# Hybrid attention and gMLP block: second chunk's tokens for z reloaded as rows and split, branch weights on GpSimd's queue, transposes moved, z's tiles where w_out's rows go later

## The chip, the cores and the metric

The kernel runs on one core of a Trainium2 chip. The metric is the device time of one execution in microseconds (us). The core has five instruction queues, each in order: PE (TensorE, matmuls and transposes), DVE (VectorE), ACT (ScalarE), POOL (GpSimd) and SP (SyncE, which only issues DMA transfers here). ACT and POOL can issue DMA transfers too. A core has 16 DMA engines that all queues share.

## What is computed

One decoder block on 2048 tokens of 1024 channels, all in float32. Cut to what matters here:

```python
h = _rmsnorm(x, norm_pre_mix[layer])
proj = jnp.einsum('bsd,de->bse', h, w_in[layer])
q, k, v = ...                                   # 12 heads of 64, rope on q and k
u = jax.nn.gelu(proj[..., U0:Z0])               # 512 channels
z = jax.nn.gelu(proj[..., Z0:GA0])              # 512 channels
gate_a = jax.nn.sigmoid(proj[..., GA0:GB0])     # 1024 channels
gate_b = jax.nn.sigmoid(proj[..., GB0:IN_WIDTH])
y_attn = _mixer_dilated_attention(q, k, v)      # 3 patterns, joined by their log-denominators
y_gmlp = _mixer_chunked_gmlp(u, z, ...)         # u * (tril(w_spatial) @ layernorm(z) + b_spatial)
merged = (gate_a * jnp.einsum('bse,ed->bsd', y_attn, w_branch_attn[layer])
          + gate_b * jnp.einsum('bse,ed->bsd', y_gmlp, w_branch_gmlp[layer]))
y = jnp.einsum('bsd,de->bse', merged, w_out[layer])
x = x + _rmsnorm(y, norm_post_mix[layer])
...                                             # squared-ReLU MLP of width 4096
```

## The kernel before

**Numbers.** Every large product is made from operands split in two: a high part (a rounded copy) and a low part (the operand less its high part). `mm3` multiplies high x high, high x low and low x high (L95, L96, L97). `split` makes the parts with one engine for the copy (L70 on ACT, L72 on POOL) and one for the difference (L78 on DVE or POOL). With `split` a raw float32 tile becomes a tile of two planes.

**Tokens.** There are four chunks of 512 tokens, 0 to 3. The normed tokens, transposed, lie in HBM twice: as raw float32 rows (`hT_d`, called hTd, 512 KB for two of the eight channel groups) and already split into two planes (`hb_d`, called hbd, twice the bytes). `reload_h(c)` makes a tile hT_b of chunk c and returns eight loads from hbd, one for two channel groups of one plane.

**The stretch around the change.** After q, k, v, u and the first half of z come the gate products (L707) in the generator `gates`: half 1 (chunks 2 and 3) and then half 0, each in seven products per block n of weight columns, numbered i = 1 to 7. Products 1 and 2 of one n use one PSUM bank: the bank is copied to x after product 1 (L726 or L728), and product 2 is added on top of it, so PE's product 2 needs that copy done. The weights of each product come through small tiles (gr, ga, cv) that are split into "spots". Attention's units run between them on all engines, a few matmuls at a time.

The order of all this is written by hand: `filler` is one long generator that yields after every three matmuls (a step), and `steps(n)` runs n of them between other work. `with behind():` puts instructions of ACT, DVE, POOL and SP behind the last one issued so far on the same engine, so that the scheduler keeps the written order.

- `combine(c)` joins attention's three patterns for one chunk: loads (A, or cw for chunk 1), statistics (L970 to L983), scaling (L988 on ACT, L991 on DVE), two adds (L993, L994), then eight transposes on PE (L999), copies and stores. `combined(...)` advances the combines of chunks 2, 3 and 0 with pairs (steps to run first, which combine). The combine of chunk 1 (the fourth) is advanced by `todo` in the loop at the end of `attention`'s function.
- Then z of half 0: `z_chunk` for chunk 0 and then chunk 1, four blocks of 128 tokens each, eight steps for a block. Each block's gelu is L572. The loads of chunk 1's tokens are in `zin`, one issued after each step. The same loop loads and splits the six branch weights (wbraw, wb; `load_wb`, `split_wb`), at steps listed in tuples.
- Then the merges. `merge(c, ...)` multiplies attention's and gMLP's outputs (yt) with the branch weights (b), and the gates (g, loaded from HBM by `load_gate`, sigmoid L1166) with these (L1183). The rows of w_out (woraw, wo) are loaded and split in the first merge (chunk 2), each row's load waiting for the place of an earlier one. The tiles woraw2, woraw3, woraw6 and woraw7 come from a pool (ttp) that lies where z's pool (zp0) was. `sz_out` finishes the gMLP branch of a chunk (L551 on PE, L558 and L561), writing sb tiles.
- `out_block` multiplies with w_out; with the first of the four blocks of a chunk the next chunk's yt and eight of its gates are loaded.

Of the kernel before, what the change touches and what calls it, by code (L numbers as in the profile page):

```python
# [41 lines left out]
def block_kernel(ctx, tc, a, out):  # L42
# [478 lines left out]
    def spatial(zp, half):  # L521

        wsp = zp.tile([P, 4, P], F32, name=f"wsp{half}", tag="wsp")
        bsp = zp.tile([P, 4, P], F32, name=f"bsp{half}", tag="bsp")
        lngb = zp.tile([P, 2, 32], F32, name=f"lngb{half}", tag="lngb")[:, :, :4]
        ones = st.tile([P, P], F32, name=f"ones{half}", tag="ones", bufs=1)
        sp.dma_start(wsp, a["w_spatial"])
# [135 lines left out]
    def gates():  # L663
# [12 lines left out]
        for t, (half, i, n) in enumerate(seq):  # L676
# [45 lines left out]
            for _ in range(2 if half and i == 4 or t in (LAST + 5, LAST + 7) else 1):  # L722
                if ins:
                    sp.dma_start(*ins.pop(0))
            if i == 1 and half and n > 1:
                dve.tensor_copy(x, p)  # L726
            elif i == 1:
                act.activation(x, p, AF.Copy)  # L728
# [38 lines left out]
    def filler():  # L767

        for q, (wi, kind, n, half) in enumerate(queue):
# [15 lines left out]
            if kind == "z":  # L785
                if not half:
                    zin.extend(reload_h(1))
                for ci in range(2):
                    yield from paced(z_chunk(zps[half], w, half * 2 + ci))
                    if half and not ci:  # L790
                        gates_ahead()
                continue
# [264 lines left out]
    def combined(*order):  # L1057
        for n, k in order:
            steps(n)
            with behind():  # L1060
                next(cs[k])

    combined((0, 0), (4, 1), (10, 0), (3, 0), (3, 0), (2, 2), (8, 0), (0, 1), (3, 1), (3, 1), (10, 1),
             (0, 2), (3, 2), (3, 2), (10, 2))
    steps(75 - 62)
    ec.close()
# [7 lines left out]
    def load_wb(k):  # L1074
        wb_raw[k] = wp.tile([P, D], F32, name=f"wbraw{k}", tag="raw", bufs=2)
        sp.dma_start(wb_raw[k], a["w_branch"][:, k, :])

# [8 lines left out]
    while not cw:  # L1086
        steps(1)
    todo = {14: (3,), 16: (3,), 18: (3,), 28: (3,)}
    for n in range(1, 56):
        steps(1)  # L1090
        if zin:
            sp.dma_start(*zin.pop(0))
        if n in (20, 24, 30, 34, 44, 50):
            split_wb((20, 24, 30, 34, 44, 50).index(n))
        if n in (6, 9, 20, 24, 30, 34):
            load_wb((6, 9, 20, 24, 30, 34).index(n))
        if n == 48:
# [71 lines left out]
    def merge(c, yt, between, each=None):  # L1169
        cs = slice(c * 512, (c + 1) * 512)  # L1170
        mg = []
        for dt in range(KT):
# [14 lines left out]
            if c != 2:  # L1187
                load_gate(c, dt + 5, 0)
                load_gate(c, dt + 3, 1)
            if dt < KT - 1:  # L1190
                for wch in range(2):
# [308 lines left out]
    for n, c in enumerate(chunks):  # L1500
        if n:
            mg = merge(c, yt, {0: flush, 2: flush}, merge_sums if c == 0 else merge_sums_last if c == 1 else None)
        for i in range(4):
# [5 lines left out]
            if n < 3 and not i:  # L1509
                yt = load_y(chunks[n + 1])  # L1510
                for dt, wch in ((0, 0), (0, 1), (1, 0), (1, 1), (2, 0), (2, 1), (3, 0), (4, 0)):
                    load_gate(chunks[n + 1], dt, wch)
            if n == 3 and i == 1:
# [562 lines left out]
```

## Time and profile before

| | |
|---|---|
| Median of 3 runs | 2667.13 us (2666.18 to 2668.09) |
| Profiled execution | 2667.0 us, span of its instructions 2665.1 us |
| TensorE clock granted, mean | 0.993 of full speed |
| ACT, POOL busy | 41%, 45% of the span |
| DMA, mean | 198 GB/s, 528.29 MB in all |

Times within the profile count from the span's start. The stretch that the change touches lies between 535 and 560 us (the first attention units) and between 970 and 1135 us (combines, z, first merge). In a list of waits a row says: engine and operation that waited, the line, what released it, then total us, number and longest. In a timeline a row gives start, duration, engine, line, operation, output and inputs, and in brackets how long the engine had stood idle and what ended that. Rows of windows give, for each engine, busy time and instructions, then the granted TensorE clock, the mean busy share of the DMA engines and GB/s. Rows of DMA issues end with the median us from issue to landing. "issue" as a releaser means that the profile shows none.

### The profile page before, as it was taken

The page shows a single profiled execution, that of the slowest core. Times are in us where ns is not written, and L with a number is a line of the kernel's source. Part 1 is how long each engine was busy: PE and PEld are TensorE (multiplying, and loading weights), DVE is VectorE, ACT ScalarE, POOL GpSimd, SP SyncE. Part 2 cuts the span into 40 slices and gives each one's busy share as a digit, 9 for nine tenths or more (in the row PEclk, how much of TensorE's full clock was granted, in tenths as well). Part 3 has the DMA queues.
Part 4 walks back from the last instruction along what each step waited for, and adds up shares of the span by engine and source line. Part 5 has one row for each costly group of instructions (what it writes and reads, how often), then busy time and mean ns, then how long its engine had stood idle before and what let it go on. Part 6 is the DMA issues. An engine that isn't in the chain of part 4 may idle for free. (4 is left out here: it accounts for less than half of the span.)

```text
span 2665.1 us, 35494 instructions
## 1 busy us (share of the span) xinstructions
PE 2622.6 (98%) x12458; PEld 2190.0 (82%) x12458; DVE 1657.0 (62%) x2799; ACT 1085.6 (41%) x2273; POOL 1192.4 (45%) x1089
## 2 busy tenths in 40 slices
PE   9999999999999998899999999999999999999998
PEld 8888888878888877688888888888888888888886
DVE  5676665544443455755676654655437888888866
ACT  5213111244445433444445555655545333223334
POOL 0363354365455552310334563223215776676644
PEclk9999999999999999899999999999999999999999
DMA  8779768888898899743656464643343212222235
GB/s 314 284 246 327 262 228 289 296 258 256 286 294 234 242 299 315 252 152 136 213 208 258 137 229 151 214 153 119 111 154 107 87 64 79 87 87 88 87 113 211
DMA packets 389860, 528.29 MB, mean 198 GB/s; under 512 B 57073, under 2 KB 242161, under 8 KB 388658
## 3 DMA queue, kind: packets, MB, share of 16 engines
q1 hardware_dynamic: 300912, 436.03, 49.7%
q0 software_dynamic: 14992, 51.65, 5.1%
q10 hardware_dynamic: 73778, 38.35, 4.7%
q8 instruction: 98, 1.61, 0.2%
q14 instruction: 80, 0.66, 0.1%
HBM read 342.77 MB, written 183.17 MB: 197 GB/s over the span
## 5 line engine op out<-in xcount | busy, mean ns | idle before, releaser
L1927 PE MATMUL ya<-T_spots,s 128*128 128x512 f32 x1176 | 289.2, 389 | 0.7 <-ACT T_spots L70 0.6
L70 ACT ACTIVATE s<-sraw 128x768 fp32r<-128x768 f32 (+1 forms) x184 | 127.2, 696 | 330.2 <-POOL sraw L1728 155.9
L1927 PEld LDWEIGHTS ya<-T_spots,s 128*128 128x128 f32 x1176 | 220.6, 188 | 47.3 <-ACT T_spots L70 1.0
L78 DVE TENSOR_TENSOR s<-sraw,s 128x512 fp32r<-128x512 f32 x172 | 184.2, 1095 | 8.6 <-ACT s L70 5.9
L1399 PE MATMUL aa<-B,A 128*128 128x512 f32 x768 | 182.2, 390 | 0.3 <-ACT xs L1413 0.3
L1370 POOL TENSOR_TENSOR s<-w1r 128x512 f32<-128x512 f32 x32 | 43.2, 1351 | 309.5 <-DVE S L78 271.8
L707 PE MATMUL g<-opA,spots 128*128 128x512 f32 x672 | 171.9, 400 | 0.0
L1399 PEld LDWEIGHTS aa<-B,A 128*128 128x128 f32 x768 | 143.9, 188 | 30.7 <-ACT xs L1413 1.0
L707 PE MATMUL g<-opB,spots 128*128 128x512 f32 x648 | 165.6, 400 | 0.0
L1927 PE MATMUL yc<-T_spots,s 128*128 128x512 f32 x624 | 159.6, 389 | 0.0
L95 PE MATMUL x<-hT_a,wq 128*128 128x512 f32 x384 | 149.7, 390 | 0.0
L96 PE MATMUL x<-hT_a,wq 128*128 128x512 f32 x384 | 149.4, 389 | 0.0
L97 PE MATMUL x<-hT_a,wq 128*128 128x512 f32 x384 | 149.4, 389 | 0.0
L707 PEld LDWEIGHTS g<-opA,spots 128*128 128x128 f32 x672 | 122.2, 190 | 22.1
L1927 PEld LDWEIGHTS yc<-T_spots,s 128*128 128x128 f32 x624 | 117.1, 188 | 24.3
L707 PEld LDWEIGHTS g<-opB,spots 128*128 128x128 f32 x648 | 118.0, 190 | 21.5
L78 POOL TENSOR_TENSOR spots<-gr,spots 128x512 fp32r<-128x512 f32 x98 | 126.6, 1295 | 17.7 <-ACT spots L70 8.3
L70 ACT ACTIVATE hl<-r 128x512 fp32r<-128x512 f32 x48 | 30.4, 633 | 235.3 <-POOL r L321 89.0
L1727 POOL TENSOR_TENSOR sraw<-sraw 128x256 f32<-128x256 f32 x56 | 41.9, 747 | 161.6 <-DVE s L78 158.6
L958 DVE TENSOR_REDUCE o<-po 128x256 f32<-128x512 f32 x48 | 33.2, 692 | 130.0 <-PE po L957 130.0
L72 POOL TENSOR_SCALAR spots<-gr 128x512 fp32r<-128x512 f32 x86 | 53.4, 621 | 133.8 <-PE g L707 96.2
L78 POOL TENSOR_TENSOR T_spots<-w2r,T_spots 128x512 fp32r<-128x512 f32 x70 | 104.5, 1520 | 7.3 <-ACT T_spots L70 7.3
(426 smaller groups left out, 6964.1 us busy)
## 6 DMA issues: line engine op xcount, KB each, us to landing
w1r<-in_w_mlp_in_dram SPq DMA_DIRECT2D x64, 512.0 KB, 3.7
sraw<-sd SPq DMA_DIRECT2D x128, 256.0 KB, 3.2
qk<-hl SPq DMA_DIRECT2D x24, 1024.0 KB, 5.6
qq<-qk SPq DMA_DIRECT2D x96, 256.0 KB, 5.1
w2r<-in_w_mlp_out_dram SPq DMA_DIRECT2D x16, 1024.0 KB, 7.6
sd<-u ACTq DMA_DIRECT2D x63, 256.0 KB, 3.1
g<-gated SPq DMA_DIRECT2D x58, 256.0 KB, 3.9
gr<-sgd SPq DMA_DIRECT2D x53, 256.0 KB, 4.7
```

Source lines behind the costliest of these rows:

```text
L70: act.activation(hi, src, AF.Copy)
L72: pool.tensor_scalar(hi, src, 1.0, 1.0, op0=OP.mult, op1=OP.mult)
L78: (pool if lo_eng == "pool" else dve).tensor_sub(lo, src, f32(hi))
L95: pe.matmul(ps, lh, rh, start=start, stop=False)
L96: pe.matmul(ps, lh, rl, start=False, stop=False)
L97: pe.matmul(ps, ll, rh, start=False, stop=stop)
L707: pe.matmul(p, w[:, l, k], h[:, r, k], start=i in (1, 6, 5, 4) and not k and not m, stop=k == 3 and m == 2, skip_group_check=True)
L958: dve.tensor_reduce(ot[:, :, j * 64:(j + 1) * 64], po.rearrange("p (b h e) -> p b e h", b=4, h=2), axis=AX.X, op=OP.add)
L1370: pool.tensor_add(s1, a21, a22)
L1399: pe.matmul(p, w[:, l, k, :], h[:, r, k, :], start=i in (1, 6, 5) and not k and not n, stop=k == 3 and n == 2, skip_group_check=True)
L1727: pool.tensor_add(a22, a21, a22)
L1927: pe.matmul(p, s[:, l], w[r], start=i in (1, 2, 5) and not m and not o, stop=m == 1 and o == 2, skip_group_check=True)
```

## The change

```diff
--- before.py
+++ after.py
@@ -523,6 +523,9 @@
         wsp = zp.tile([P, 4, P], F32, name=f"wsp{half}", tag="wsp")
         bsp = zp.tile([P, 4, P], F32, name=f"bsp{half}", tag="bsp")
         lngb = zp.tile([P, 2, 32], F32, name=f"lngb{half}", tag="lngb")[:, :, :4]
+        if not half:
+            zp.tile([P, 512], F32, name="sb_place", tag="sz", bufs=5)
+            zp.tile([P, 512], F32, name="ur_place", tag="ur", bufs=4)
         ones = st.tile([P, P], F32, name=f"ones{half}", tag="ones", bufs=1)
         sp.dma_start(wsp, a["w_spatial"])
         sp.dma_start(lngb[:, 0, :], a["ln_v_gain"])
@@ -722,9 +725,7 @@
             for _ in range(2 if half and i == 4 or t in (LAST + 5, LAST + 7) else 1):
                 if ins:
                     sp.dma_start(*ins.pop(0))
-            if i == 1 and half and n > 1:
-                dve.tensor_copy(x, p)
-            elif i == 1:
+            if i == 1:
                 act.activation(x, p, AF.Copy)
             elif i == 2:
                 act.activation(z, p, fn)
@@ -784,7 +785,8 @@
             w = loaded[q]
             if kind == "z":
                 if not half:
-                    zin.extend(reload_h(1))
+                    hT[1] = hp.tile([P, 2, KT, 512], F32R, name="hT_b1", tag="hT", bufs=2)
+                    zin.extend((f32(hT[1])[:, 1, k:k + 2], hT_d[1][:, k:k + 2]) for k in range(0, KT, 2))
                 for ci in range(2):
                     yield from paced(z_chunk(zps[half], w, half * 2 + ci))
                     if half and not ci:
@@ -1060,9 +1062,9 @@
             with behind():
                 next(cs[k])
 
-    combined((0, 0), (4, 1), (10, 0), (3, 0), (3, 0), (2, 2), (8, 0), (0, 1), (3, 1), (3, 1), (10, 1),
-             (0, 2), (3, 2), (3, 2), (10, 2))
-    steps(75 - 62)
+    combined((0, 0), (4, 1), (8, 0), (3, 0), (3, 0), (2, 2), (6, 1), (3, 1), (3, 1), (1, 0),
+             (10, 2), (3, 2), (3, 2), (1, 1), (19, 2))
+    steps(75 - 69)
     ec.close()
     ega.close()
 
@@ -1073,7 +1075,7 @@
 
     def load_wb(k):
         wb_raw[k] = wp.tile([P, D], F32, name=f"wbraw{k}", tag="raw", bufs=2)
-        sp.dma_start(wb_raw[k], a["w_branch"][:, k, :])
+        pool.dma_start(wb_raw[k], a["w_branch"][:, k, :])
 
     def split_wb(k):
         with behind():
@@ -1085,15 +1087,19 @@
     next(sg)
     while not cw:
         steps(1)
-    todo = {14: (3,), 16: (3,), 18: (3,), 28: (3,)}
+    todo = {22: (3,), 24: (3,), 27: (3,), 38: (3,)}
     for n in range(1, 56):
         steps(1)
         if zin:
             sp.dma_start(*zin.pop(0))
-        if n in (20, 24, 30, 34, 44, 50):
-            split_wb((20, 24, 30, 34, 44, 50).index(n))
-        if n in (6, 9, 20, 24, 30, 34):
-            load_wb((6, 9, 20, 24, 30, 34).index(n))
+        if n in (12, 15, 18, 21):
+            k, h = (n - 12) // 3 * 2, hT[1]
+            with behind():
+                split(h[:, 0, k:k + 2], h[:, 1, k:k + 2], f32(h)[:, 1, k:k + 2], "act", "pool")
+        if n in (24, 28, 32, 36, 42, 48):
+            split_wb((24, 28, 32, 36, 42, 48).index(n))
+        if n in (4, 6, 25, 29, 33, 37):
+            load_wb((4, 6, 25, 29, 33, 37).index(n))
         if n == 48:
             next(sg)
         for k in todo.get(n, ()):
@@ -1187,6 +1193,9 @@
             if c != 2:
                 load_gate(c, dt + 5, 0)
                 load_gate(c, dt + 3, 1)
+            elif dt > 2:
+                load_gate(c, dt + 2, 1)
+                load_gate(c, dt + 3, 0)
             if dt < KT - 1:
                 for wch in range(2):
                     open_gate(c, dt + 1, wch)
@@ -1509,7 +1518,8 @@
             if n < 3 and not i:
                 yt = load_y(chunks[n + 1])
                 for dt, wch in ((0, 0), (0, 1), (1, 0), (1, 1), (2, 0), (2, 1), (3, 0), (4, 0)):
-                    load_gate(chunks[n + 1], dt, wch)
+                    with behind():
+                        load_gate(chunks[n + 1], dt, wch)
             if n == 3 and i == 1:
                 e2r.close()
                 egx.close()
```

In words: the copy of PSUM after product 1 is made by ACT for all n. Chunk 1's tokens for z come as four raw loads from hTd into the low plane, 2 MB and not 4; ACT copies each to the high plane and POOL takes the difference. The steps of the first three combines' transposes and of the fourth combine are other ones. The branch weights' loads are issued by POOL. In zp0 two names take places ahead, so that z's tiles lie elsewhere. In the first merge gates are loaded two or three blocks ahead from dt = 3; the next chunk's gates go behind yt's loads on SP.

The instructions change places on three engines as follows. Lines of the changed kernel are higher by 2 to 6.

ACT in the first attention units, around the copies gx and ga (n = 2, 3 and 4 are gx_4403, ga_4526 and ga_4527; nm and e are attention's exponentials). Before:

```order
L70 ACTIVATE spots_4204<-gr_4205 128x512 x2
L70 ACTIVATE spots_4204<-gr_4206 128x512 x2
L730 ACTIVATE gz<-g_4426 128x512
L730 ACTIVATE gz<-g_4461 128x512
L70 ACTIVATE opB<-opB 128x1024
L909 ACTIVATE nm_4607<-o_4063 128x4
L912 ACT_TABLE_LOAD
L912 ACTIVATE e_4592,o_4063<-e_4592,nm_4607 128x128
L912 ACTIVATE e_4592,o_4063<-e_4592,nm_4607 128x256 x3
L730 ACTIVATE gz<-g_4562 128x512
```

With the change:

```order
L70 ACTIVATE spots_4204<-gr_4206 128x512 x2
L729 ACTIVATE gx_4403<-g_4461 128x512
L70 ACTIVATE opB<-opB 128x1024
L731 ACTIVATE gz<-g_4426 128x512
L729 ACTIVATE ga_4526<-g_4562 128x512
L731 ACTIVATE gz<-g_4461 128x512
L70 ACTIVATE opB<-opB 128x1024
L911 ACTIVATE nm_4607<-o_4063 128x4
L914 ACT_TABLE_LOAD
L914 ACTIVATE e_4592,o_4063<-e_4592,nm_4607 128x128
L914 ACTIVATE e_4592,o_4063<-e_4592,nm_4607 128x256 x3
L729 ACTIVATE ga_4527<-g_4624 128x512
```

The copy for n = 2 now stands behind four spots, the one for n = 4 behind nm and the four exponentials. DVE had these copies between its sb and e instructions.

DVE in z, at the fourth combine (cw) and the first branch weight (wb). Before:

```order
L978 TENSOR_TENSOR Z_9694<-E_9689,cw 128x4x4 x3
L979 TENSOR_TENSOR M_9686<-Z_9694 128x16
L980 TENSOR_TENSOR M_9686<-M_9686,Z_9694 128x16
L981 RECIPROCAL M_9686<-M_9686 128x16
L983 TENSOR_TENSOR E_9689<-E_9689,M_9686 128x4x4 x3
L991 TENSOR_TENSOR cw<-cw,E_9689 128x4x256 x2
L993 TENSOR_TENSOR cw<-cw 128x4x256
L994 TENSOR_TENSOR cw<-cw 128x4x256
L574 BN_STATS bs_9761<-z_9621 128x6
L575 BN_AGGR mv_9622<-bs_9761 128x2
L78 TENSOR_TENSOR wb_9594<-wbraw_9651,wb_9594 128x1024
```

With the change:

```order
L981 TENSOR_TENSOR M_9721<-Z_9729 128x16
L78 TENSOR_TENSOR wb_9594<-wbraw_9645,wb_9594 128x1024
L982 TENSOR_TENSOR M_9721<-M_9721,Z_9729 128x16
L983 RECIPROCAL M_9721<-M_9721 128x16
L985 TENSOR_TENSOR E_9724<-E_9724,M_9721 128x4x4 x3
L577 BN_STATS bs_9800<-z_9623 128x6
L993 TENSOR_TENSOR cw<-cw,E_9724 128x4x256
L578 BN_AGGR mv_9624<-bs_9800 128x2
L993 TENSOR_TENSOR cw<-cw,E_9724 128x4x256
L104 TENSOR_SCALAR v_ln_9805<-mv_9624 128x4
L995 TENSOR_TENSOR cw<-cw 128x4x256
L996 TENSOR_TENSOR cw<-cw 128x4x256
```

wb's first difference (L78) stood behind cw's two adds and a block's statistics (L574); now it stands between the two sums of cw's statistics, ahead of all of cw's large products, and z's statistics stand among these.

POOL from the last gate weights to yt. Before:

```order
L532 AFFINE_SELECT wsp_9603<-wsp_9603 128x128 x4
L72 TENSOR_SCALAR wb_9594<-wbraw_9651 128x1024
L72 TENSOR_SCALAR wb_9595<-wbraw_9669 128x1024
L72 TENSOR_SCALAR wb_9596<-wbraw_9749 128x1024
L72 TENSOR_SCALAR wb_9597<-wbraw_9770 128x1024
L72 TENSOR_SCALAR wb_9598<-wbraw_9808 128x1024
L72 TENSOR_SCALAR wb_9599<-wbraw_9845 128x1024
L72 TENSOR_SCALAR yt_10005<-yt_10005 128x512
L78 TENSOR_TENSOR yt_10005<-yt_10005 128x512
```

With the change:

```order
L535 AFFINE_SELECT wsp_9603<-wsp_9603 128x128 x4
L78 TENSOR_TENSOR hT_b_9622<-hT_b_9622 128x1024 x4
L72 TENSOR_SCALAR wb_9594<-wbraw_9645 128x1024
L1078 DMA wbraw_9773<-in_w_branch_dram 128x1024
L72 TENSOR_SCALAR wb_9595<-wbraw_9653 128x1024
L1078 DMA wbraw_9791<-in_w_branch_dram 128x1024
L72 TENSOR_SCALAR wb_9596<-wbraw_9773 128x1024
L1078 DMA wbraw_9828<-in_w_branch_dram 128x1024
L72 TENSOR_SCALAR wb_9597<-wbraw_9791 128x1024
L1078 DMA wbraw_9844<-in_w_branch_dram 128x1024
L72 TENSOR_SCALAR wb_9598<-wbraw_9828 128x1024
L72 TENSOR_SCALAR wb_9599<-wbraw_9844 128x1024
```

Four differences of hT_b stand ahead of wb's first copy, and a load of a branch weight (L1078) stands ahead of four of the wb copies; each of these loads waits for DVE to be done with an earlier wbraw.

## The prediction

> **What bounds the kernel now.** I read the page's busy times first, then the waits of PE over the whole span, then windows of 5 us around those waits.
>
> ```profile
> PE 2622.6 (98%) x12458; PEld 2190.0 (82%) x12458; DVE 1657.0 (62%) x2799; ACT 1085.6 (41%) x2273; POOL 1192.4 (45%) x1089
> ```
> ```profile
> PE yt L999 <- issue: 9.3, 3, 3.2
> PE b L95 <- DVE g L1183: 5.7, 2, 5.0
> PE g L707 <- DVE ga L726: 4.3, 1, 4.3
> PE b L96 <- POOL yt L78: 3.7, 4, 1.3
> PE z L97 <- DMA hT_b<-hbd: 1.8, 1, 1.8
> ```
> ```profile
> core 0: us, PE busy (x) PEld busy (x) DVE busy (x) ACT busy (x) POOL busy (x), PEclk, DMA share, GB/s
> 550.00:555.00 5.00, 5.00 (x13) 3.90 (x12) 0.74 (x3) 3.92 (x11) 1.32 (x2) 0.51 0.75 226
> 1005.00:1010.00 5.00, 5.00 (x18) 4.00 (x16) 1.65 (x7) 2.44 (x4) 0.70 (x2) 0.66 0.97 317
> 1085.00:1090.00 5.00, 4.23 (x14) 3.46 (x15) 4.16 (x5) 0.63 (x1) 2.13 (x2) 0.50 0.94 328
> 1125.00:1130.00 5.00, 3.71 (x9) 2.94 (x10) 4.55 (x7) 4.21 (x8) 0.53 (x1) 0.50 0.64 200
> ```
>
> PE sets the time. The change adds and removes no matmul, so it can only move the waits of the second list, 24.8 us together, and what follows them: after four of these places the granted clock falls to about one half (0.51, 0.66, 0.50, 0.50). A window at 0.66 has lost 0.34 x 5 = 1.7 us, one at 0.50 2.5 us. So the stakes are some 35 us of 2665.
>
> **A, the copies from PSUM (L726).** Six go from DVE to ACT.
>
> ```profile
> 546.24 2.05 DVE L561 TENSOR_TENSOR sb<-sb,ur 128x512 f32<-128x512 f32 x1
> 548.22 0.68 DVE L726 COPY ga<-g 128x512 f32<-128x512 f32 x1
> 549.04 3.33 PE L707 MATMUL g<-hT_a,spots 128*128 128x512 f32 x7 [4.27 <-DVE ga L726]
> 537.23 1.41 ACT L70 ACTIVATE spots<-gr 128x512 fp32r<-128x512 f32 x2 [0.76 <-DMA gr<-in_w_in_dram]
> 553.75 0.19 ACT L912 ACTIVATION_READ_ACCUMULATOR e<-e,nm 128x1 f32 x1
> ```
>
> The copy that PE waits for at 549.04 stood on DVE behind the sb work. On ACT it can run at about 541, so those 4.27 us go. But two neighbours get later: the copy for n=2 stands behind the spots that end at 538.64 (PE waits about 1.1 us), the one for n=4 behind nm and the four exponentials, which end near 553.9; PE would be there at about 552.2 (wait 1.7). In the run before, PE came to that product at half clock, about 558.3. Gain 4.2 us (2.5 if the new waits bring the half clock back, 5.5 if ACT starts its exponentials earlier).
>
> **B, the transposes of the combines.** A step is three matmuls, 0.68 us at 0.227 us each. From the statistics to the transposes there were 16 steps, 10.9 us, and PE still waited about 3 us: the chain needs 14.
>
> ```profile
> 974.45 1.08 DVE L970 TENSOR_TENSOR M<-A 128x16 f32<-128x16 f32 x1 [2.82 <-DMA A<-att]
> 986.14 1.22 DVE L994 TENSOR_TENSOR A<-A 128x1024 f32<-128x1024 f32 x1
> 987.46 1.07 PE L999 MATMUL yt<-ident,A 128*128 128x128 f32 x8 [2.96 <-issue]
> ```
>
> The view calls the releaser "issue", but DVE's add ended at 987.36 each time just ahead of it. Now the distances are 21, 27 and 26 steps, 14.3, 18.4 and 17.7 us. The second and third wait vanish. For the first, the start is fixed by a landing (974.45), so the add stays at 987.36; PE comes 9 matmuls, 2.0 us, later, at 986.5: 0.9 us are left. Together 8.4 us of waits, and 2 x 1.7 us of half clock after the first two: z would begin 11.8 us earlier, at 1018.2 and not 1029.99.
>
> **C, z's tokens and weights take it back.**
>
> ```profile
> 1036.46 0.50 PE L97 MATMUL z<-w_z,hT_b 128*128 128x512 f32 x1 [1.77 <-DMA hT_b<-hbd]
> 995.00:1036.50 41.50, 33.42 (x148) 26.91 (x146) 24.90 (x38) 14.66 (x42) 15.55 (x12) 0.96 0.87 291
> hT_b<-hbd SPq DMA_DIRECT2D x15, 512.0 KB, 6.6
> ```
>
> z already waits for the last piece of its first tokens. That load is in its old place on SP's queue, behind the same loads and stores; the smaller reload of the second chunk comes after it. The transfers of 995 to 1036.5 are 0.87 x 41.5 = 36.1 us of full DMA time, and one branch weight (512 KB, 1.4 us at the 366 GB/s of a saturated window) is added to them by POOL's queue. Even without a gap they end at 1032.5 if they start at 995, at 1029 if SP's stores come free 3.5 us sooner with B's gain. PE needs the piece at 1022.7. I take a landing at 1031: a new wait of 8 us and 2.5 us of half clock behind it. Against 1036.46, B and C together give 5.5 - 2.5 = +3 us (from -1, with 1034 and a long half-clock stretch, to +7).
>
> **The last combine and the branch weights.** Four differences (hT_b) and the first wb copy now stand ahead on POOL, and the first wb difference stands on DVE within the last combine's chain.
>
> ```profile
> L78 POOL TENSOR_TENSOR opB<-opB x12: 2385/2396/2791, 531.0 to 948.8; 128x1024 fp32r<-128x1024 f32 x12
> L72 POOL TENSOR_SCALAR wb<-wbraw 128x1024 fp32r<-128x1024 f32 x6 | 7.0, 1167 | 25.6 <-DMA wbraw<-in_w_branch_dram 25.6
> 1051.96 0.60 ACT L572 ACTIVATE z<-z 128x512 f32<-128x512 f32 x1
> 1046.81 2.48 DVE L991 TENSOR_TENSOR cw<-cw,E 128x1024 f32<-128x1024 f32 x2
> 1049.33 1.22 DVE L993 TENSOR_TENSOR cw<-cw 128x1024 f32<-128x1024 f32 x1
> 1050.68 1.23 DVE L994 TENSOR_TENSOR cw<-cw 128x1024 f32<-128x1024 f32 x1
> ```
>
> Count from s24, when PE ends z's 24th step (its third block). ACT: gelu 0.6, two hT_b copies of 1.06 (the duration of such a copy in the last fence). POOL: the differences are bounded by opB's, 2.4 to 2.8 us; the last ends at s24+6.5, wb's copy at 7.7. DVE: wb's difference at 9.0, then E (0.35), the cw work (4.9) and three small ones of z between (1.0): s24+15.3. PE reaches the transposes, now 15 steps after s24, at s24+10.2. A new wait of 5.1 us, where before there was none.
>
> The row 979.78 of the view below shows that cw's kind of product can also take longer, 3.43 us a pair. The Trainium skill (GPSIMD Engine Reference, section 1, Specifications) says that GpSimd shares its SBUF interface with a VectorE instruction of two SBUF inputs; by it the copy of wb1 that runs beside would stretch the chain by about 1 us, and the sum would be 1 us lower.
>
> ```profile
> 979.78 3.43 DVE L991 TENSOR_TENSOR A<-A,E 128x1024 f32<-128x1024 f32 x2
> 1073.40 1.05 POOL L72 TENSOR_SCALAR wb<-wbraw 128x1024 fp32r<-128x1024 f32 x1 [5.17 <-DMA wbraw<-in_w_branch_dram]
> 1074.78 1.41 POOL L72 TENSOR_SCALAR yt<-yt 128x512 fp32r<-128x512 f32 x1 [0.33 <-issue]
> 1085.77 0.80 PE L96 MATMUL b<-yt,wb 128*128 128x512 f32 x1 [1.30 <-POOL yt L78]
> wbraw<-in_w_branch_dram SPq DMA_DIRECT2D x6, 512.0 KB, 4.6
> ```
>
> **D, the split of yt on POOL.** It begins after wb's last copy, and the product's last wait for it ends 11.0 us later. Before, s24 was 1029.99 + 24 x 0.68 + 1.77 = 1048.1, so D ended at s24+37.7. Now POOL issues the last four wbraw loads itself, each waiting for DVE to finish with the buffer, and its queue stands meanwhile. wb1's difference comes behind cw: s24+16.5. Then a load (4.6), copy and difference (2.3), a load (0.5 + 4.6) and a copy: POOL is free at s24+29.7, D ends at s24+41.0. That is 3.3 us later; the wait at the transposes is inside it, since D's wait shrinks by as much. With a little half clock on both sides I take -3.5 us (0 if POOL's differences run by 2 us a piece, -8 if the half clock comes twice).
>
> **E, w_out's rows.** z's tiles now lie where the third and fourth row go (woraw2, woraw3), so these wait for little.
>
> ```profile
> 1117.01 0.53 POOL L1122 DMA_DIRECT2D woraw<-in_w_out_dram  x1 [8.18 <-DVE mg L78]
> 1118.70 0.63 ACT L1166 ACTIVATE g<-g 128x512 f32<-128x512 f32 x1 [3.60 <-DMA g<-gated]
> 1123.32 1.06 ACT L70 ACTIVATE wo<-woraw 128x1024 fp32r<-128x1024 f32 x1 [2.51 <-DMA woraw<-in_w_out_dram]
> 1124.41 1.23 DVE L78 TENSOR_TENSOR wo<-woraw,wo 128x1024 fp32r<-128x1024 f32 x1 [2.26 <-ACT wo L70]
> 1125.55 1.88 DVE L1183 TENSOR_TENSOR g<-g,b 128x512 f32<-128x512 f32 x3
> ```
>
> PE waits 5.0 us until 1126.29 for the first of those three products, which stands on DVE behind wo, ACT's copy and the row issued at 1117.01. That row now goes out about 9 us earlier, and the gate that ACT waits for until 1118.70 stands behind the other row's copy. The product is then due near 1120.5, before PE wants its bank (1121.3). Gain 5 us and 2 of the some 3 us of half clock: +7 (3 if the gate's landing at 1118.7 is late, 8 at best). The other gates, moved behind yt, and the swapped loads of ga10 and cv0 I cost at nothing: attention's and merge's PE work covers them; were a spot late, about 1 us each.
>
> **Sum.** 4.2 + 3 - 3.5 + 7 = 10.7 us. The profiled execution took 2667.0 us (span 2665.1), the median is 2667.13, so the shift is 0.1: 2656 us. Half-clock stretches are the loosest part. The rows show them after waits of 2.96 and 3.14 us and not after the 3.17 us of the third transposes; the Trainium skill (TensorE: Matmul & The Clock Gate, "Part 1: The HAM clock gate") explains this with a free-running window of about 3.4 us. By that page the remaining 1 us waits would leave the clock full, and the new ones of 5 and 8 us surely would not; the sum stays, with about 2 us either way.
>
> **Rivals.** First, the DMA does not bind z: the transfers of the first tokens close up, since 0.87 left gaps and not all of the 36.1 us is ahead of z. Then C is hidden and B+C give 11.8 + 1.8 = 13.6: 2667.1 - 21.3 = 2646 us. Against it: shares of 0.9 to 1.0 in the windows. Second, **slower**: POOL's in-order queue, at b's first products. If a wbraw load takes the 7 to 10 us of a saturated stretch (hT_b's 6.6, below it) and not 4.6, two of them in series cost up to 10.8 more; the differences at 2.8 us add 1.6, the chain's stretch 1, the half clock 3.4. D then loses 3.5 + 16.8 = 20.3 against the 14.2 of A, B, C and E: 2673 us. It decides from about 8 us a load. For it: POOL's issue waits inside its own queue; against it: the DMA has room from 1065 on and 2 MB less to carry. Third, C and D take all: z starts 1031 + 4 late, the wait at the transposes adds instead of moving, and about 2666 us comes out, no change.
>
> **How the numbers follow.** Forecast 0.47, first rival 0.14, slower 0.23, no change 0.16. A measurement of this kernel tells about 0.2%, 5.3 us, from no change: faster 0.61, same 0.16, slower 0.23. The forecast's own range is 2649 to 2662; to leave out no more than two in ten it reaches to both rivals: 2642 to 2675.
>
> **What would show it.** Right: no wait at g (n=3), transposes of the first three combines waiting 1 us or less, z waiting 6 to 10 us for hT_b or w_z, cw's transposes 4 to 6 us, b's first products for POOL until about s24+41, and nothing over 1 us for DVE in the merge. Wrong: z starting near 1018 and running through, or POOL's wbraw issues standing more than 8 us each.

## The result and the profile after

The changed kernel takes 2662.62 us (median of 20 runs, 2658.43 to 2665.16) where the kernel before takes 2667.71 us (20 runs): ratio 0.9981, 95% interval 0.9974 to 0.9988. That is 5.1 us faster, half of the 10.7 us forecast. Run twice more beside the kernel before, it gave 0.9991 (0.9981 to 1.0001) and 0.9988 (0.9979 to 0.9997), so 3 to 5 us. The profiled execution took 2663.1 us, its span 2661.4.

PE still sets the time. Its busy time on the page, and its waits over the whole span (engine, operation and line, what ended the wait; total us, number, longest):

```profile
PE 2619.8 (98%) x12458; PEld 2186.9 (82%) x12458; DVE 1665.8 (63%) x2793; ACT 1090.9 (41%) x2283; POOL 1207.1 (45%) x1099
```
```profile
PE yt L1001 <- issue: 6.3, 1, 6.3
PE z L95 <- DMA hT_b<-hbd: 4.2, 1, 4.2
...
PE b L95 <- DVE g L1189: 2.1, 2, 1.1
PE o L95 <- ACT mg L70: 1.9, 2, 1.4
PE b L96 <- POOL yt L78: 1.9, 3, 1.3
PE g L710 <- DVE cv L742: 1.9, 1, 1.9
PE g L710 <- ACT ga L729: 1.6, 1, 1.6
```

The old list is turned over. The three waits of yt, 9.3 us, are gone, and so are the 4.3 us for DVE's copy; the 5.0 us in the first merge has become 1.1. In their place stand one wait of 6.3 us at yt (the fourth combine's transposes), 4.2 us of z for its tokens, and small new ones at cv, ga and mg.

Since PE runs the same matmuls, one instruction's start can be compared in the two profiles. The difference is how far the changed kernel is ahead at that place:

```
PE instruction                   before     after   difference   since the last   forecast
first gate product               517.20    516.47      -0.73         -0.73
gate product behind A            561.82    556.30      -5.52         -4.79          -4.2
z's first                       1029.99   1015.66     -14.33         -8.81
z's, behind three blocks        1048.39   1040.07      -8.32         +6.01     (B+C) -3
b's first behind D              1092.93   1089.75      -3.18         +5.14          +3.5
o's first                       1133.04   1123.74      -9.30         -6.12          -7
o's 97th                        1154.80   1147.49      -7.31         +1.99
last of the program             2654.64   2650.44      -4.20         +3.11           0
```

B and C together give -8.81 + 6.01 = -2.80. Up to o's first product the change is 9.3 us ahead, near the forecast, and it loses 5.1 us behind that, where nothing was forecast. The two new long waits, in timelines of PE (start, duration, operation; in brackets how long PE stood idle and what ended it), and the windows behind them:

```profile
1024.77 0.77 PE L95 MATMUL z<-w_z,hT_b 128*128 128x512 f32 x1 [4.20 <-DMA hT_b<-hbd]
1056.73 1.94 PE L1001 MATMUL yt<-ident,cw 128*128 128x128 f32 x8 [6.30 <-issue]
```
```profile
1025.00:1030.00 5.00, 4.36 (x10) 2.98 (x11) 0.66 (x1) 0.60 (x1) 0.00 (x0) 0.51 1.06 385
1055.00:1060.00 5.00, 3.27 (x12) 3.01 (x13) 4.72 (x9) 1.68 (x4) 1.63 (x2) 0.50 0.21 12
```

After each of them the granted clock (the first figure behind POOL's) is 0.5.

The small wait of 1.9 us at cv costs more than its length, too: behind it the clock is at 0.50 for 3.41 us (the last row of the last view), half of which, 1.7 us, is lost.

```profile
980.91 3.11 PE L710 MATMUL g<-opA,spots 128*128 128x512 f32 x9 [1.86 <-DVE cv L742]
```

What holds the fourth combine's transposes back is seen in timelines of DVE, POOL and ACT:

```profile
1036.48 2.40 DVE L973 TENSOR_TENSOR M<-M,cw 128x16 f32<-128x16 f32 x1
1038.91 2.50 DVE L976 TENSOR_TENSOR E<-cw,M 128x16 f32<-128x16 f32 x3
1044.35 3.35 DVE L980 TENSOR_TENSOR Z<-E,cw 128x16 f32<-128x16 f32 x3 [2.12 <-ACT E L977]
1047.72 1.23 DVE L78 TENSOR_TENSOR wb<-wbraw,wb 128x1024 fp32r<-128x1024 f32 x1
1049.35 1.70 DVE L985 TENSOR_TENSOR E<-E,M 128x16 f32<-128x16 f32 x3
1055.40 1.23 DVE L996 TENSOR_TENSOR cw<-cw 128x1024 f32<-128x1024 f32 x1
```
```profile
1036.45 4.75 POOL L78 TENSOR_TENSOR hT_b<-hT_b 128x1024 fp32r<-128x1024 f32 x2 [4.45 <-ACT hT_b L70]
1041.89 4.75 POOL L78 TENSOR_TENSOR hT_b<-hT_b 128x1024 fp32r<-128x1024 f32 x2 [0.69 <-ACT hT_b L70]
1046.62 1.07 POOL L72 TENSOR_SCALAR wb<-wbraw 128x1024 fp32r<-128x1024 f32 x1
```
```profile
1040.76 2.00 ACT L70 ACTIVATE hT_b<-hT_b 128x1024 fp32r<-128x1024 f32 x2
1044.07 0.24 ACT L977 ACTIVATE E<-E 128x48 f32<-128x48 f32 x1
```

M, E and Z are tiny: 16 numbers a partition. One product for M takes 2.40 us, three for E 2.50 and three for Z 3.35, while POOL forms differences of hT_b (2.38 us each). The Trainium skill (Trainium Architecture — The Big Picture, section "What this means for kernel authors") calls the port that DVE and GpSimd share an exclusive lock, not a split of bandwidth; the 2.40 us of one small DVE product beside POOL's 2.38 agree with it.

Two chains meet here. On DVE, E waits for its exponential on ACT, which stands behind two copies of hT_b until 1044.07, and Z ends at 1047.70. On POOL, wb's copy stands behind the four differences and ends at 1047.69. The difference of wb (1047.72), which now stands in the combine's order on DVE, needs both. Either chain alone would have held wb's difference until the same moment. What the shared port adds can be read only behind it, where E's three products take 1.70 us beside POOL's next copy.

### The profile page after: what moved, and what is told of

Same layout as the page of the kernel before. It is cut to its first block, busy times and chain, and to the rows that moved or that the text cites. A ratio compares the mean times of both kernels' runs of the same rounds, so it can differ in the third digit from the quotient of the medians.

```text
span 2661.4 us, 35503 instructions
## 1 busy us (share of the span) xinstructions
PE 2619.8 (98%) x12458; PEld 2186.9 (82%) x12458; DVE 1665.8 (63%) x2793; ACT 1090.9 (41%) x2283; POOL 1207.1 (45%) x1099
## 5 line engine op out<-in xcount | busy, mean ns | idle before, releaser
L78 DVE TENSOR_TENSOR s<-sraw,s 128x512 fp32r<-128x512 f32 x172 | 184.1, 1095 | 8.5 <-ACT s L70 8.5
L78 POOL TENSOR_TENSOR spots<-gr,spots 128x512 fp32r<-128x512 f32 x98 | 127.5, 1304 | 22.7 <-DMA gr<-in_w_in_dram 15.7
L78 POOL TENSOR_TENSOR T_spots<-w2r,T_spots 128x512 fp32r<-128x512 f32 x70 | 104.4, 1519 | 7.3 <-ACT T_spots L70 7.3
```

Source lines behind the costliest of these rows:

```text
L78: (pool if lo_eng == "pool" else dve).tensor_sub(lo, src, f32(hi))
```

## The experiments

Ratios are to the kernel before on the same chip, with their 95% interval. "The trace moves" means the starts of the same PE instructions against the first profile of the changed kernel, so that what happened ahead of the edit is taken off. Two unaltered repeats (experiment 10) move against the first profile as well: by up to 2 us in each stretch from z to the first merge, by 1.1 and 3.4 us in the merge, and by 2.9 us either way behind it. Moves of that size are not told from chance.

**1. The copies on DVE again.**

```diff
-            if i == 1:
+            if i == 1 and half and n > 1:
+                dve.tensor_copy(x, p)
+            elif i == 1:
                 act.activation(x, p, AF.Copy)
```

> The changed kernel with the copies of PSUM after product 1 (n > 1, first half) on DVE again. Theory (each term of the sum reaches the end): the 4.3 us wait for DVE's copy and the half clock behind it return, 4.9 us slower than the changed kernel, about 2667.5 us. Rival (z's first products wait for a landing that does not depend on PE, which swallows what was won ahead of it): at most 1 us slower, about 2663, with z's wait for hT_b near 1 us and not 5.

Measured: 1.0010 (1.0002 to 1.0018), 2671.9 us. The trace moves by 5.0 us at the place (7.02 us behind ahead of it, 11.99 after), and PE waits as before:

```profile
PE g L710 <- DVE ga L729: 4.4, 1, 4.4
...
PE z L95 <- DMA hT_b<-hbd: 3.9, 1, 3.9
```

z's wait is no shorter for it (3.5 to 4.2 us in the three profiles of the changed kernel), though z starts 10.9 us later: the landing has moved with PE, so a gain far ahead of z passes through. That SP's queue, which follows PE's progress, is the reason was not tested by itself. The theory holds.

**2. The old steps of the transposes.**

```diff
-    combined((0, 0), (4, 1), (8, 0), (3, 0), (3, 0), (2, 2), (6, 1), (3, 1), (3, 1), (1, 0),
-             (10, 2), (3, 2), (3, 2), (1, 1), (19, 2))
-    steps(75 - 69)
+    combined((0, 0), (4, 1), (10, 0), (3, 0), (3, 0), (2, 2), (8, 0), (0, 1), (3, 1), (3, 1), (10, 1),
+             (0, 2), (3, 2), (3, 2), (10, 2))
+    steps(75 - 62)
```

> The changed kernel with the old steps of the first three combines' transposes. Theory (the DMA takes back most of what the later transposes win): three waits of some 3 us return, z's wait for hT_b falls from 5.2 to 2 us or less, 2.8 us slower, about 2665.4 us. Rival (the later transposes are worth what the trace shows at z's start, 8.8 us): about 2671 us.

Measured: 1.0005 (0.9994 to 1.0016). PE's waits from 980 to 1060 us, ahead of the fourth combine's transposes:

```profile
PE yt L1001 <- issue: 11.1, 3, 5.0
PE z L97 <- DMA hT_b<-hbd: 0.3, 1, 0.3
```

Three waits are back and z's wait for its tokens has gone. At z's start the trace is 12.5 us further behind (16.07 against 3.54), after z's first blocks 5.8 (9.29). So the DMA takes back more than half, 6.7 us; the size of what is left is between the two numbers, since one of the three waits came back as 5.0 us and not 3.1.

**3. Without the places in z's pool.**

```diff
-        if not half:
-            zp.tile([P, 512], F32, name="sb_place", tag="sz", bufs=5)
-            zp.tile([P, 512], F32, name="ur_place", tag="ur", bufs=4)
```

> The changed kernel without the two places ahead in z's pool, so w_out's third and fourth row wait for z's tiles again. Theory: the wait of 5 us of b for DVE in the first merge returns and the 1.4 us wait of o for ACT's mg goes, 4.2 us slower, about 2666.8 us. Rival (the order of the gates alone removed that wait): no change, 2662.6 us.

Measured: 0.9990 (0.9982 to 0.9999). b waits for DVE 4.8 us in four pieces, none over 1.6:

```profile
PE b L95 <- DVE g L1186: 4.8, 4, 1.6
```

The trace moves by 2.1 us there, which is within chance, and the same waits are 2.1, 3.9 and 3.3 us in the three profiles of the changed kernel. The time does not decide: 4.2 us slower would be 0.9997, no change 0.9981 to 0.9991, and the interval reaches both. But the one wait of 5 us did not return, so the order of the gates keeps it away without the places, as the rival had it.

**4. The fourth combine's transposes later.**

```diff
-    todo = {22: (3,), 24: (3,), 27: (3,), 38: (3,)}
+    todo = {22: (3,), 24: (3,), 27: (3,), 52: (3,)}
```

> The changed kernel with the transposes of the fourth combine 14 steps later (52 and not 38). Theory: the 6.3 us wait of PE there goes, but the first products of b then wait for POOL's split of yt until the same moment, since POOL's chain of differences, branch weights and yt has not moved; 1.5 us faster at most, about 2661 us, with waits of b for POOL of 6 us or more. Rival (that wait is the chain's only cost): 8 us faster, 2655 us.

Measured: 0.9987 (0.9978 to 0.9995), no faster. The 6.3 us are gone, and b waits for POOL:

```profile
PE b L95 <- POOL yt L72: 4.5, 1, 4.5
PE z L95 <- DMA hT_b<-hbd: 3.9, 1, 3.9
PE b L96 <- POOL yt L78: 3.4, 3, 1.4
```

At z the trace is 1 to 2 us ahead, past the transposes' old place 9.6 us ahead, and after b's first products 1.1 us behind. A wait taken away ahead of a later one on the same chain wins nothing: the theory holds, the rival falls.

**5. The tokens loaded from hbd again.**

```diff
-                    hT[1] = hp.tile([P, 2, KT, 512], F32R, name="hT_b1", tag="hT", bufs=2)
-                    zin.extend((f32(hT[1])[:, 1, k:k + 2], hT_d[1][:, k:k + 2]) for k in range(0, KT, 2))
+                    zin.extend(reload_h(1))
...
-        if n in (12, 15, 18, 21):
-            k, h = (n - 12) // 3 * 2, hT[1]
-            with behind():
-                split(h[:, 0, k:k + 2], h[:, 1, k:k + 2], f32(h)[:, 1, k:k + 2], "act", "pool")
```

> The changed kernel with the second chunk's tokens loaded from hbd again (eight loads of two planes, no copies on ACT, no differences on POOL). Theory (POOL's four differences lock DVE's small operations and put wb and yt back): the 6.3 us wait at the fourth combine's transposes falls to 1 us or less, M, E and Z of that combine take 0.2 to 0.5 us on DVE again and not 2 to 3, the waits of b for POOL shrink; 4 to 6 us faster than the changed kernel, ratio to before about 0.9960. Rival (the 2 MB that the reload saves are worth more): z's second chunk waits 3 us or more for hT_b and the kernel is 2 us slower than the changed one, 0.9990 or more.

Measured: 0.9958 (0.9943 to 0.9973), 2657.1 us: 6 to 9 us faster than the changed kernel. DVE in this run, where POOL forms no differences:

```profile
1034.31 0.17 DVE L972 TENSOR_TENSOR M<-M,cw 128x16 f32<-128x16 f32 x1
1034.52 0.35 DVE L975 TENSOR_TENSOR E<-cw,M 128x16 f32<-128x16 f32 x3
1035.18 0.35 DVE L979 TENSOR_TENSOR Z<-E,cw 128x16 f32<-128x16 f32 x3 [0.31 <-ACT E L976]
```

0.17 us and not 2.40, 0.35 and not 2.50 and 3.35. No wait at the transposes is left, and z's second chunk does not wait for the 2 MB more. The theory's time holds and the rival falls; the waits of b for POOL did not shrink (2.6 us, 1.9 in the changed kernel). The edit takes away the shared port, POOL's order and the copies on ACT together, so it does not tell which of them held the combine.

**6. The gates in the old order.**

```diff
-            elif dt > 2:
-                load_gate(c, dt + 2, 1)
-                load_gate(c, dt + 3, 0)
...
-                    with behind():
-                        load_gate(chunks[n + 1], dt, wch)
+                    load_gate(chunks[n + 1], dt, wch)
```

> The changed kernel with the gates' loads in their old order (none ahead in the first merge, the next chunk's ahead of yt's on SP). Theory (the gate ahead of ACT's third copy of w_out was the larger part of E, the places the smaller): b waits 3 us or more for DVE in the first merge, some 3 us slower than the changed kernel, ratio about 0.9992. Rival (the gates' order costs: it brings the waits of o for mg and the small ones behind it): 2 to 4 us faster, 0.9970 or less.

Measured: 0.9978 (0.9967 to 0.9988), not told from the changed kernel; the theory's 0.9992 lies outside, the rival's 0.9970 within. A wait of b of 4.0 us is back, and yet the end is not later:

```profile
PE b L95 <- DVE g L1189: 5.4, 2, 4.0
```

The trace loses 3.5 us in the first merge (0.61 us ahead to 2.94 behind) and has 2.8 of them back at aa (1429 us, 0.14 behind). An unaltered repeat lost 3.4 us in the merge and had 2.9 back behind it, so the order's own worth is not shown by this.

**7 to 9. The branch weights earlier.** `best_a` is experiment 5 with

```diff
-        if n in (24, 28, 32, 36, 42, 48):
-            split_wb((24, 28, 32, 36, 42, 48).index(n))
-        if n in (4, 6, 25, 29, 33, 37):
-            load_wb((4, 6, 25, 29, 33, 37).index(n))
+        if n in (8, 10, 16, 20, 26, 30):
+            split_wb((8, 10, 16, 20, 26, 30).index(n))
+        if n in (4, 6, 9, 11, 17, 21):
+            load_wb((4, 6, 9, 11, 17, 21).index(n))
```

> As the run without the reload, and the branch weights loaded and split earlier (splits at steps 8, 10, 16, 20, 26, 30). Theory: POOL is through with them before yt, so the waits of b for POOL go as well, and the fourth combine's chain is alone on DVE: 9 to 11 us faster than the changed kernel, ratio to before about 0.9942. Rival (DVE or the DMA takes it back, the loads now share the stretch in which the DMA is full): z waits longer for hT_b, at most 3 us faster, 0.9970.

Measured: 0.9969 (0.9958 to 0.9980). b no longer waits for POOL, but four of wb's differences now stand ahead of the combine on DVE, which begins at 1043.96, and the transposes wait 6.3 us for DVE (L995): DVE takes it back, as the rival said, and its number was met. The combine begins some 10 us later than in experiment 5, so DVE's order makes most of this wait; its two adds, beside POOL's split of yt, also take 1.62 and 2.10 us and not 1.2.

`best_b` keeps the reload from hTd, has wb early and the transposes at step 52.

> The changed kernel with the branch weights early (as in the last one), the reload from hTd kept, and the fourth combine's transposes at step 52. Theory: no wait at those transposes and none of b for POOL: 8 to 10 us faster than the changed kernel, ratio about 0.9946. Rival (POOL's chain still ends too late for the first products, as with the later transposes alone): no faster, 0.9981.

Measured: 0.9978 (0.9966 to 0.9990); the theory missed, and the rival has the time without its mechanism. Even at step 52 the transposes come too early, since four of wb's differences (the last two at 1048.57 and 1056.46 us) stand ahead of the combine on DVE:

```profile
PE yt L1001 <- DVE cw L996: 7.6, 1, 7.6
```

`best_c` is `best_a` with the transposes at step 52.

> The run without the reload from hTd, with the branch weights early and the fourth combine's transposes at step 52. Theory (each wait of the stretch from z to the first merge has its own cause, and these three edits take the causes of two): no wait at the transposes, none of b for POOL, 3 us faster than the run without the reload alone, ratio to before about 0.9947. Rival (POOL's split of yt, now beside the combine's products on DVE, stretches them past step 52): a wait of 3 us or more there, ratio 0.9958 or more.

Measured: 0.9941 (0.9925 to 0.9957), 2652.8 us, the fastest of all, some 16 us under the kernel before and 14 under the changed one measured beside it (2666.7). Its interval overlaps that of experiment 5, so the theory's 3 us over that run are not shown. Its waits:

```profile
PE va L95 <- DVE vt L357: 4.9, 1, 4.9
PE z L95 <- DMA hT_b<-hbd: 3.9, 1, 3.9
PE b L95 <- DVE g L1184: 3.8, 3, 2.9
```

Neither yt nor b for POOL is left. From z to the first merge its trace gains 13.0 us on the changed kernel (6.60 behind to 6.45 ahead). In the merge, where b waits for DVE again, it loses some 3 us, as the unaltered repeat does.

**10. The changed kernel again, twice.**

> The changed kernel once more, unaltered. Theory (the waits behind the first merge, at b, o and aa from 1354 us on, are not made by the change): in this profile at least one of them differs by 0.5 us or more from the first profile of the changed kernel, ratio to before 0.9981 within 0.001. Rival (they belong to the change): the same waits, each within 0.2 us.

> The changed kernel unaltered, beside the last. Its ratio to before lies between 0.9981 and 0.9991, the two so far, and the waits of PE from z to the first merge are within 0.3 us of the first profile's, those behind it and those ahead of 560 us not.

Measured: 0.9991 and 0.9988, as above. In the first of them the wait of o for mg was 0.4 us and not 1.4, and aa did not wait for ACT's xs, as the theory had it; in the second z waits 3.5 and not 4.2 us for the tokens, outside the 0.3 us expected, and o 1.9. One wait of b for DVE in the merge, 1.0 us in the first profile, is 2.3 and 2.2 in the repeats. Another one moves in front of everything: va for vt, at 238 us, was below 0.3 us in the first profile, 2.0 in this second repeat and 4.9 in `best_c`, though all edits lie behind it:

```profile
PE va L95 <- DVE vt L357: 2.0, 1, 2.0
```

So the three profiles of one program have spans of 2661.4, 2661.1 and 2665.6 us, 4.5 us apart, and a gain of 5 us is told by medians over many runs, not by one trace.

**11. The branch weights' loads on SP again.**

```diff
-        pool.dma_start(wb_raw[k], a["w_branch"][:, k, :])
+        sp.dma_start(wb_raw[k], a["w_branch"][:, k, :])
```

> The changed kernel with the branch weights' loads on SP's queue again, at the same steps. Theory (each load waits for DVE to free its buffer, whichever queue holds it, and POOL has nothing else to do meanwhile): within 2 us of the changed kernel, ratio 0.9978 to 0.9988, and the transposes still wait some 6 us. Rival (POOL's queue standing behind its own loads is what made its chain late): the waits of b for POOL go, 3 to 4 us faster, 0.9968.

Measured: 0.9969 (0.9957 to 0.9980), 5.6 us faster than the changed kernel measured beside it (0.9991), so the theory's 2 us were missed and the rival's 0.9968 was met. The transposes wait 6.4 us as before; b waits 1.0 us for POOL and not 1.9, and from z to the last product the trace gains 3.6 us (1.51 behind to 2.05 ahead), little more than chance. POOL's own loads do cost, in the way of the rival, but most of the difference is not accounted for in the trace.

**12. Neither edit of the first merge** (3 and 6 together).

> The changed kernel without either of the two edits of the first merge: no places in z's pool, gates in the old order. Each alone cost 1 to 3 us there by its trace and less at the end. Theory (what the first merge gains is handed on to waits behind it, at o, b and aa, and half or more is lost there): a wait of b for DVE of 4 us or more returns, and the end is 1 to 3 us slower than the changed kernel of the same call. Rival (the 7 us of the prediction are right, and something else lost time): 5 us or more slower.

Measured: 0.9993 (0.9983 to 1.0003), beside 0.9988 (0.9979 to 0.9997) of the changed kernel: 1.5 us slower by the medians. The two intervals together allow from 2 us faster to 5 us slower, and not 7.

```profile
PE b L95 <- DVE g L1186: 6.7, 3, 5.4
```

The trace loses 5.7 us in the merge (6.81 to 12.55) and has 3.6 of it back by the last product (8.93): 5.7 us gained by the two edits, 2.1 kept. From b's products behind D to o's first it loses 7.0 us against the first profile of the changed kernel, 3.7 and 5.9 against the repeats. The rival, the forecast's 7 us at the end, falls. That half or more is handed on fits the first profile and is not told from chance.

**13. `best_c` with the branch weights on SP's queue.**

> The fastest run so far (no reload from hTd, branch weights split early, last transposes at step 52) with the branch weights' loads on SP's queue, where they stand behind the second chunk's tokens. Theory (1 MB less ahead of z's first tokens, 2.8 us at 366 GB/s): z's wait for hT_b falls from some 4.5 to 2 or 3 us and the branch weights are still in time; 1 to 3 us faster than that run, ratio to before about 0.9933. Rival (loaded so late they make yt late): waits of b for POOL return, 2 us or more slower, 0.995.

Measured: 0.9970 (0.9959 to 0.9981), a miss on both sides: z's wait stayed at 4.2 us, and nothing of yt was late. On SP the weights stand behind the second chunk's tokens, so four of their differences reach DVE late, just ahead of the combine, which begins at 1057.41 and not, as in experiment 5, at 1034:

```profile
1050.04 1.22 DVE L78 TENSOR_TENSOR wb<-wbraw,wb 128x1024 fp32r<-128x1024 f32 x1
1052.54 1.22 DVE L78 TENSOR_TENSOR wb<-wbraw,wb 128x1024 fp32r<-128x1024 f32 x1
1056.27 1.23 DVE L78 TENSOR_TENSOR wb<-wbraw,wb 128x1024 fp32r<-128x1024 f32 x1 [1.91 <-POOL wb L72]
1057.41 0.17 DVE L971 TENSOR_TENSOR M<-cw 128x16 f32<-128x16 f32 x1
```

PE waits for it:

```profile
PE yt L1000 <- DVE cw L995: 8.4, 1, 8.4
```

## Why the prediction was right or wrong

**Right in its places.** Every wait above 2 us that the change made was named: z for hT_b (4.2 us in one piece, 5.2 in all, where 6 to 10 were named), cw's transposes (6.3 for 4 to 6) and b for POOL. So were those that went. The terms below are read from the first profile; the repeats show how far each can be trusted (us since the last row, against the kernel before):

```
up to                             first    second     third   forecast
first gate product                -0.73     -0.17     +2.07          0
gate product behind A             -4.79     -3.62     -4.85       -4.2
z's, behind three blocks (B+C)    -2.80     -3.39     -5.30         -3
b's first behind D                +5.14     +3.21     +5.21       +3.5
o's first (E)                     -6.12     -2.76     -5.00         -7
last of the program               +5.10     +2.25     +7.93          0
```

- **A**: 4.2 us forecast, 4.8 in the trace, 5.0 in experiment 1. The wait for ga (n = 4) was put at 1.7 us and is 1.6; the one for gx (n = 2) at 1.1, and is 0.2 to 1.4.
- **B and C**: +3 forecast, 2.8 found. B's three waits went, but the forecast of z's start, 1018.2 less A's 4.2, so 1014.0, was met 1.7 us late: the first combine comes earlier on DVE, and the product from which cv is made (980.09) now stands behind its 3.43 us product (974.33). No term had that wait and its half clock, 1.9 + 1.7 us. C was sized at 8 us of waiting and 2.5 of half clock, and came as 5.2 (0.4, 4.2 and 0.6 us, the last up to 1026.6 and not 1031) and 2.3. B gave 3.0 us less than forecast (8.8 for 11.8) and C took some 3 us less, so the sum is right by luck and its parts are not. Experiment 2 shows the kind as forecast, z's transfers taking back 6.7 of 12.5 us.
- **The fourth combine**: 5.1 us forecast, 6.3 found. The chain on POOL was right to 0.1 us up to wb's difference (s24 + 8.9, with s24 at 1040.07), though the stretched M, E and Z, which end at the same moment, were not in it; then E took 1.70 us and not 0.35 beside POOL, and the chain ended at s24 + 16.6 and not 15.3. The sentence on the shared port, by which the wait would be 1 us longer, was nearer than the sum without it.
- **D**: its end was put at s24 + 41.0 and came at 44.0 (1084.07). The second of the four loads in POOL's queue stood 7.25 us for DVE, behind the late combine (the 11.0 us of the prediction's text are 11.3 by its rows, 1074.45 to 1085.77, and its sum goes by these):

```profile
1058.18 0.58 POOL L1078 DMA_DIRECT2D wbraw<-in_w_branch_dram  x1 [7.25 <-DVE t_ln L110]
1063.26 0.58 POOL L1078 DMA_DIRECT2D wbraw<-in_w_branch_dram  x1 [3.42 <-DVE wb L78]
```

  Combine and D together cost 5.1 us and not 3.5 (3.2 and 5.2 in the repeats). Experiment 4 shows, as forecast, that D takes in the wait ahead of it.

**Wrong in E.** The step that failed is "Gain 5 us and 2 of the some 3 us of half clock: +7", with the nothing that the sum puts behind the merge. The merge gained 6.1 us in the first profile, 2.8 and 5.0 in the repeats, and 5.1, 2.2 and 7.9 us were lost behind it. The text asked only when b's bank comes free, and not what stands next: o's first products need mg, whose copies on ACT stand among copies of yt that wait for a load of their own:

```profile
1128.20 0.63 ACT L70 ACTIVATE yt<-yt 128x512 fp32r<-128x512 f32 x1 [1.51 <-DMA yt<-yad]
1128.74 0.61 ACT L70 ACTIVATE mg<-g 128x512 fp32r<-128x512 f32 x1
```

PE waits twice for mg, 1.9 us (0.4 and 1.9 in the repeats), and 2.0 us are given back from o's first to its 97th product. In experiment 6, where PE comes to o 3.5 us later and does not wait, this copy runs at 1128.67 all the same, and only 1.9 of the 3.5 us are left behind it: what PE wins ahead of the copy is in part lost at it. More went at b (1354 us), o and aa, where the kernel before had smaller waits or none. Experiment 12 measures the term: 5.7 us gross, net 1.5 by the medians and 2.1 by the trace, and at most 5 with the intervals. With 2 for 7 and 5.1 for 3.5 the forecast would have been 4.1 us, and 3 to 5 were measured. That E was priced too high is shown. Where its gain goes is shown for mg in part alone: the waits behind the merge change from one profile of the same program to the next, and which of them take it in a given run was not settled.

**What no term priced**: the reload from hTd by itself. Its parts were costed at nothing apart from the combine and D; undone alone it gives 6 to 9 us, more than the whole change gave. The bytes it saves were of no use, since the tokens from hbd were in time (experiment 5). The second rival, slower by POOL's queue, had the right engine: its loads took 5.0 us at the median and 7.1 at most, less than the 8 us from which it decides. Whether POOL's differences did harm through the shared port or through POOL's order the runs do not tell apart, since both chains end at 1047.7 us.

## What to carry to other kernels

Price a saved wait at what the next one on the same chain leaves of it: ask when the operand of the product behind it is ready, and take only the lesser of the two. Before work is moved to POOL, list the small DVE instructions that run beside it, since each can wait out a whole POOL instruction. Fewer bytes help only where a wait ends on their landing; here eight loads of split planes beat four of raw rows, since the splitting stood on ACT and POOL ahead of what the next products waited for.

## What the runs showed of the hardware

Products of 128x16 on DVE took 0.17 us with POOL idle and 2.40 us beside a difference of 128x1024 on POOL that takes 2.38; three in a row took 2.50 to 3.35 us against 0.35.

The fall of the clock does not follow the length of the wait. The kernel before and experiment 2 both wait 3.17 us at the third transposes; in the first the clock stays at 1.00 behind it, in the second it falls. In the changed kernel it falls behind 1.86 us at cv. In every trace the stretches at half clock begin on one grid of 3.41 us, and all but the one at the program's end last whole steps of it (in the kernel before 988.38 to 991.80, and five steps later 1005.45 to 1008.86). Here are rows along this grid, for the kernel before, experiment 2 and the changed kernel: the window in which PE waits, and the next one.

```profile
1019.10:1022.52 3.42, 1.62 (x12) 1.52 (x13) 2.30 (x3) 0.95 (x2) 0.00 (x0) 1.00 0.86 176
1022.52:1025.93 3.41, 3.41 (x17) 2.81 (x16) 0.69 (x1) 1.42 (x2) 0.00 (x0) 1.00 1.02 408
```
```profile
1019.37:1022.78 3.41, 1.19 (x10) 1.18 (x11) 2.71 (x4) 0.52 (x2) 0.00 (x0) 1.00 0.87 162
1022.78:1026.20 3.42, 3.42 (x10) 2.65 (x9) 0.00 (x0) 1.84 (x3) 0.00 (x0) 0.50 1.02 393
```
```profile
978.74:982.15 3.41, 1.55 (x8) 1.06 (x7) 3.34 (x9) 3.11 (x4) 0.00 (x0) 1.00 1.07 388
982.15:985.56 3.41, 3.41 (x14) 2.92 (x13) 3.31 (x12) 2.12 (x9) 0.54 (x1) 0.50 1.09 367
```

PE was idle for 1.80 us of the first window, 2.22 of the second and 1.86 of the third, and the clock fell behind the last two. In the sixteen traces, from 30 us on, it fell behind each of the 54 windows at full clock in which PE was idle for 1.85 us or more, behind 7 of the 32 with 1.56 to 1.84 us, and behind none with less. So a wait of 2 us can cost 1.7 us more, and one of 3 us, cut in two by the grid, nothing. By these figures a wait of 3.7 us or more, twice 1.85, is sure to be followed by half clock wherever the grid cuts it.

The Trainium skill (TensorE: Matmul & The Clock Gate, "Part 1: The HAM clock gate") has the clock fall after an idle window of about 3.4 us that runs freely, not started by the wait. The traces agree with a window of 3.41 us that has a phase of its own. They do not agree that it must be idle from end to end: 1.86 of 3.41 us was enough.
